# Second half's value products by query halves into two banks, and the first half's turn into the banks of the main products

## The chip, the cores and the metric

The kernel runs on one core of one Trainium2 chip. Its time is the device time in microseconds (us) of one execution; below it, all times are from one execution that the hardware profiler recorded, counted from its first instruction. TensorE (PE) multiplies and writes to PSUM, which has eight banks of 512 float32 values in each of 128 partitions; VectorE (DVE) and ScalarE (ACT) read PSUM and write SBUF; GpSimd (POOL) and SyncE (SP) mostly issue transfers.

## The reference

A trunk of two layers over 256 tokens of width 2048: a Mamba-2 layer, then a layer of sliding-window attention with a sink per head. Only the attention is touched by the change:

```python
WINDOW = 128; ATT_HEADS = 32; KV_HEADS = 4; ATT_HEAD_DIM = 64
qb = q.reshape(bsz, nb, WINDOW, hk, rq, hd)                      # nb = 2 blocks of 128 tokens
kk = concat([previous block's keys, own keys]); vv = likewise    # 256 keys a block
s = einsum("bcqhrd,bckhd->bchrqk", qb, kk) * hd ** -0.5
diff = (arange(128)[:, None] + 128) - arange(256)[None, :]
valid = (diff >= 0) & (diff < WINDOW) & (key exists)
s = where(valid, s, -inf)
m = maximum(max(s), sink); p = exp(s - m)
p = p / (sum(p) + exp(sink - m))
o = einsum("bchrqk,bckhd->bcqhrd", p, vv)
return (o * silu(gate)) @ w_out
```

A token sees itself and the 127 tokens before it. So a query of the second block (tokens 128 to 255) sees exactly 128 keys: query i of the block sees keys i+1 to 127 of the first block and keys 0 to i of its own. For the queries 0 to 63 of the block no key above 63 of the own block counts, and for the queries 64 to 127 no key below 64 (in truth 65) of the first.

## The kernel before

All large products keep float32 accuracy by splitting both operands into a high and a low float32r part and adding three products (`mac`, `out_unit`, `x_stat`; lines L248, L319 to L321, L972). Weights stream in by SyncE's queue as units of 128 x 2048 values; ScalarE makes the high part (`wh`, L160) and VectorE the low part (`wl`, L163). Main products write to PSUM tiles of the pool `mm`, which has four banks that rotate; everything else (turns, scores, value products) writes to the pool `ax`, with the other four. A new tile takes the bank of the tile four places earlier in its pool and so waits for that tile's readers.

The attention layer works by four head groups j (one key/value head, eight query heads) and two halves h of the tokens (`attend`). The order of large blocks is written out in `B_ORDER`: q product, gate product and output product of the groups, q and gate of group 1 ahead of the output of group 0 and so on. The attention steps are hung between the main products by `later(n, fn)`, which runs a step n units of main products later; on each engine the instructions then keep the order that a scheduler gives them. For one group and half the steps are:

- q is turned (`qtr`, L1050) into `qT`, with two heads above each other in the 128 partitions.
- Scores (L1087): the two heads of a partition pair are products with 64 rows, `par` 0 in rows 0 to 63 and `par` 1 in rows 64 to 127, into two ax tiles. The first half takes two ax tiles (four heads each, 128 keys). The second half takes four (two heads each, 256 keys).
- For the second half, ScalarE copies the own block's scores to `p` (L1101), and VectorE puts the first block's over them where the own key lies in the future (L1102). So `p` holds 128 keys a query, each at its place in one block or the other. Softmax follows on VectorE and ScalarE.
- `turn_p` turns `p` by 128 x 128 transposes (L1127), four to a PSUM tile. For the first half a tile is copied out, one by VectorE (L1138) and one by ScalarE (L1136). For the second half VectorE writes it twice, masked by `anti` (first block's keys) and by `tri` (own keys) (L1131).
- `pv` multiplies values and turned `p` (L1145), 64 output columns to a product, `par` 0 to partitions 0 to 63 and `par` 1 to partitions 64 to 127 of one ax tile, over 512 moving columns (four heads x 128 queries). The first half has two such products, the second half four, two by blocks of keys. VectorE multiplies with the gate (L1151), ScalarE and VectorE split the result (L1160, L1161) for the output product.

In groups 0 to 2 the second half's scores come directly behind the first half's turn on TensorE; in group 3 the first half's turn comes later, directly ahead of the second half's turn. The second half's value products stand ahead of the next group's `qtr` in groups 0 to 2, and directly behind the first half's in group 3.

The values `vt` and the turned `p` are plain float32, and such a product shows as two matmul records in the trace.

Of the kernel before, what the change touches and what calls it, by code (L numbers as in the profile page):

```python
# [8 lines left out]
F32 = mybir.dt.float32  # L9
# [5 lines left out]
ALU = mybir.AluOpType  # L15
AX = mybir.AxisListType

P = 128
# [63 lines left out]
def trunk(ctx: ExitStack, tc: tile.TileContext, A: dict, out: bass.AP, dbg=None):  # L82
    nc = tc.nc
    PSUM = bass.MemoryType.PSUM

    def pool(name, bufs=1, side=None, space=None, stack=ctx):
        kw = {"space": space} if space is not None else {}
        return stack.enter_context(
            tc.tile_pool(name=name, bufs=bufs, side=side, reuse_waits="tile", **kw)
        )  # L90
# [9 lines left out]
    def nm(s):  # L100
        uid[0] += 1
        return f"{s}_{uid[0]}"

    def mm_tile():
        return mm_ps.tile([P, 512], F32, tag="mm", name=nm("mm"), bufs=4)

    def ax_tile():
        return ax_ps.tile([P, 512], F32, tag="ax", name=nm("ax"), bufs=4)
# [145 lines left out]
    def later(n, fn):  # L254
        pending.append([n, fn])
# [547 lines left out]
    for g in range(NG):  # L803
        t = 10 * g
# [136 lines left out]
    bp = pool("bp")  # L941
# [38 lines left out]
    vt = bp.tile([P, 2, S], F32, tag="vt", name="vt")  # L980
# [49 lines left out]
    sg = {}  # L1030
# [44 lines left out]
    def attend(j, h):  # L1075


        nk = P * (h + 1)
        q2 = qT[j, h]
        p = bp.tile([P, 8, P], F32, tag=f"p{h}", name=nm("p"), bufs=1)  # L1080
        per = 512 // nk
        for b in range(0, 4, per):
            pss = [ax_tile(), ax_tile()]
            for i in range(per):
                for par in range(2):
                    rows = slice(64 * par, 64 * par + 64)
                    nc.tensor.matmul(  # L1087
                        pss[par][:, i * nk : (i + 1) * nk], q2[rows, b + i, :], kT[rows, j, :nk],
                        start=True, stop=True,
                    )  # L1090
            for par in range(2):
                v = p[:, par * 4 + b : par * 4 + b + per, :]
                if h == 0:
                    nc.vector.tensor_tensor(
                        v, pss[par][:].rearrange("p (a k) -> p a k", a=per),
                        mask_a0.unsqueeze(1).to_broadcast([P, per, P]), ALU.add,
                    )
                    continue
                two = pss[par][:].rearrange("p (a c k) -> p a c k", a=per, c=2)

                nc.scalar.copy(v, two[:, :, 1, :])  # L1101
                nc.vector.copy_predicated(  # L1102
                    v, mask_a0.bitcast(U32).unsqueeze(1).to_broadcast([P, per, P]), two[:, :, 0, :]
                )
        sk = snk[:, j * 8 : j * 8 + 8]
        sm = bp.tile([P, 8, 8], F32, tag="sm", name=nm("sm"), bufs=2)
        mx, ng, rs, es, ri = [sm[:, i, :] for i in range(5)]
        nc.vector.tensor_reduce(mx, p[:], AX.X, ALU.max)
        nc.vector.tensor_tensor(mx, mx, sk, ALU.max)
        nc.vector.tensor_scalar(ng, mx, -1.0, None, ALU.mult)  # L1110
        nc.vector.tensor_tensor(es, sk, ng, ALU.add)
        nc.scalar.activation(es, es, AF.Exp)
        for r in range(8):
            nc.scalar.activation(
                p[:, r, :], p[:, r, :], AF.Exp, bias=ng[:, r : r + 1], accum_out=rs[:, r : r + 1]
            )
        nc.vector.tensor_tensor(rs, rs, es, ALU.add)
        nc.vector.reciprocal(ri, rs)
        nc.vector.tensor_tensor(p[:], p[:], ri.unsqueeze(2).to_broadcast([P, 8, P]), ALU.mult)

        pts = {}

        def turn_p():
            for par in range(2):
                pt = ax_tile()
                for a in range(4):
                    nc.tensor.transpose(pt[:, a * P : (a + 1) * P], p[:, par * 4 + a, :], ident)  # L1127
                for kc in range(h + 1):
                    t = bp.tile([P, 512], F32, tag="pt", name=nm("pt"), bufs=NPT)
                    if h:  # L1130
                        nc.vector.tensor_tensor(  # L1131
                            t[:].rearrange("p (a q) -> p a q", a=4), pt[:].rearrange("p (a q) -> p a q", a=4),
                            (anti, tri)[kc].unsqueeze(1).to_broadcast([P, 4, P]), ALU.mult,
                        )
                    elif par:
                        nc.scalar.copy(t[:], pt[:])  # L1136
                    else:
                        nc.vector.tensor_copy(t[:], pt[:])  # L1138
                    pts[kc, par] = t

        def pv():
            ov = ax_tile()
            for kc in range(h + 1):
                for par in range(2):
                    nc.tensor.matmul(  # L1145
                        ov[64 * par : 64 * par + 64, :], vt[:, kc, j * 64 : j * 64 + 64], pts[kc, par][:],
                        start=kc == 0, stop=kc == h,
                    )
            o = bp.tile([P, 4, P], F32, tag="o", name=nm("o"), bufs=1)
            hs = slice(h * P, (h + 1) * P)  # L1150
            nc.vector.scalar_tensor_tensor(  # L1151
                o[:], ov[:].rearrange("p (a t) -> p a t", a=4), 0.5, sg[j][:, :, hs], ALU.mult, ALU.mult
            )
            if j not in os_:
                os_[j] = (
                    bp.tile([P, 4, S], F32R, tag="oH", name=nm("oH"), bufs=2),
                    bp.tile([P, 4, S], F32R, tag="oL", name=nm("oL"), bufs=2),
                )
            oH, oL = os_[j]
            nc.scalar.activation(oH[:, :, hs], o[:], AF.Copy)  # L1160
            nc.vector.tensor_tensor(oL[:, :, hs], o[:], oH[:, :, hs].bitcast(F32), ALU.subtract)  # L1161


        last = j == 3
        later(4 if last and h == 0 else 3, turn_p)
        later((5 if last else 6) if h == 0 else (8 if 0 < j < 3 else 4), pv)
        if h == 0:
            later(1 if last else 3, lambda: attend(j, 1))
# [193 lines left out]
```

## Time and profile before

| | us |
|---|---|
| median of 3 runs (lowest, highest) | 998.05 (997.94, 998.2) |
| span of the profiled execution | 996.5 |
| TensorE busy (its share of the span) | 990.9 (99%) |
| VectorE busy | 771.6 (77%) |
| ScalarE busy | 567.2 (57%) |
| GpSimd busy | 106.4 (11%) |
| score products L1087, 128 records | 14.7 |
| value products L1145, 48 records | 11.8 |
| transposes of p L1127, 64 records | 8.3 |

For the profiled execution the profile gives the span, from the first to the last instruction, and no other time of its own; the runs' times include what lies around the span, 1.55 us by the median. Busy times of TensorE count each record with its drain, and records overlap: a better measure of what a group costs is the time from its first start to the start of the next line's first record. In the timeline, consecutive records of one line are merged, with their count behind an x. "128*64 128x512" is a product with 128 rows and 64 columns of the array and 512 moving columns.

### The profile page before, as it was taken

The numbers are of one execution on the slowest core, as the hardware profiler recorded it, in microseconds if no ns is written. First come the engines' busy times: TensorE is split into PE (matmuls) and PEld (weight loads), VectorE is DVE, ScalarE is ACT, GpSimd is POOL, SyncE is SP. The second block draws the span as 40 slices with busy tenths as digits, with TensorE's granted clock in tenths as the row PEclk, the third lists the DMA queues.
The fourth block names the chain that finished last, engine by engine and source line by source line (L and its number), as shares of the span: only waits on it lengthen the run. The fifth ranks groups of instructions, "written<-read, shape, count | busy, mean of one in ns | idle before, by whom it ended". The sixth has DMA issues, their size and how long they took to land.

```text
span 996.5 us, 17887 instructions
## 1 busy us (share of the span) xinstructions
PE 990.9 (99%) x7036; PEld 899.3 (90%) x7036; DVE 771.6 (77%) x1186; ACT 567.2 (57%) x992; POOL 106.4 (11%) x130
## 2 busy tenths in 40 slices
PE   9999999999999999999999999999999999999998
PEld 8999989999999998999999999888988878978976
DVE  7888897867886886786786787898688776676686
ACT  7595856547646645664654764565545544544542
POOL 0001202004003003000300300403000000000003
PEclk9999999999999999999999999999999999999999
DMA  9787587565576666656656456457664546546432
GB/s 364 250 281 300 168 275 213 183 221 178 181 243 184 222 196 192 212 191 210 207 172 227 152 188 219 169 169 244 234 199 144 177 155 192 154 150 200 133 145 84
DMA packets 61555, 198.81 MB, mean 200 GB/s; under 512 B 6848, under 2 KB 11360, under 8 KB 61216
## 3 DMA queue, kind: packets, MB, share of 16 engines
q1 hardware_dynamic: 58528, 188.47, 57.6%
q0 software_dynamic: 2336, 8.69, 2.6%
q8 instruction: 55, 0.90, 0.4%
q10 hardware_dynamic: 608, 0.52, 0.2%
q14 instruction: 28, 0.23, 0.1%
HBM read 195.43 MB, written 2.23 MB: 198 GB/s over the span
## 4 chain that ended last, share of the span: by engine, by line
PE 98%; DVE 1%; issue 0%; ACT 0%; DVEq 0%
PE mm L248 53%; PE mm L972 10%; PE mm L319 9%; PE mm L320 9%; PE mm L321 9%; PE ax L627 2%; PE ax L1087 1%; PE ax L1145 1%; PE ax L603 1%; PE ax L1127 1%; PE ax L586 0%; PE mm L386 0%; PE ax L1050 0%; PE ax L903 0%; DVE wl L163 0%; PE ax L368 0%
## 5 line engine op out<-in xcount | busy, mean ns | idle before, releaser
L163 DVE TENSOR_TENSOR wl<-wr,wh 128x1024 fp32r<-128x1024 f32 (+2 forms) x338 | 392.9, 1182 | 108.7 <-ACT wh L160 106.6
L160 ACT ACTIVATE wh<-wr 128x1024 fp32r<-128x1024 f32 (+2 forms) x338 | 332.6, 1010 | 208.4 <-issue 84.9
L248 PE MATMUL mm<-xH,wh 128*128 128x256 f32 x1280 | 355.7, 278 | 0.0
L248 PE MATMUL mm<-xL,wh 128*128 128x256 f32 x1280 | 354.4, 277 | 0.0
L248 PE MATMUL mm<-xH,wl 128*128 128x256 f32 x1280 | 354.2, 277 | 0.0
L248 PEld LDWEIGHTS mm<-xH,wh 128*128 128x128 f32 x1280 | 241.0, 188 | 1.8 <-ACT wh L194 0.5
L248 PEld LDWEIGHTS mm<-xL,wh 128*128 128x128 f32 x1280 | 241.0, 188 | 1.0
L248 PEld LDWEIGHTS mm<-xH,wl 128*128 128x128 f32 x1280 | 240.8, 188 | 0.0
L319 PE MATMUL mm<-wh,yH 128*128 128x512 f32 x256 | 101.4, 396 | 0.0
L320 PE MATMUL mm<-wh,yL 128*128 128x512 f32 x256 | 99.8, 390 | 0.0
L321 PE MATMUL mm<-wl,yH 128*128 128x512 f32 x256 | 99.7, 389 | 0.0
L643 POOL TENSOR_TENSOR yz<-yz,z 128x256 f32<-128x256 f32 x32 | 32.8, 1033 | 470.4 <-DVE yz L638 470.4
L248 PE MATMUL mm<-x1H,wh 128*128 128x256 f32 x256 | 71.7, 280 | 0.0
L490 DVE SCALAR_TENSOR_TENSOR cv<-mm,pc,cv 128x255 f32<-128x255 f32 x144 | 68.6, 477 | 3.3 <-ACT cv L488 1.9
L248 PE MATMUL mm<-x1L,wh 128*128 128x256 f32 x256 | 70.8, 277 | 0.0
L248 PE MATMUL mm<-x1H,wl 128*128 128x256 f32 x256 | 70.8, 276 | 0.0
L972 PE MATMUL mm<-wh,x1H 128*128 128x512 f32 x160 | 62.9, 393 | 0.0
L972 PE MATMUL mm<-wl,x1H 128*128 128x512 f32 x160 | 61.8, 389 | 0.0
L972 PE MATMUL mm<-wh,x1L 128*128 128x512 f32 x160 | 60.9, 390 | 0.0
L319 PEld LDWEIGHTS mm<-wh,yH 128*128 128x128 f32 x256 | 48.1, 188 | 10.3 <-DVE z L579 1.0
L321 PEld LDWEIGHTS mm<-wl,yH 128*128 128x128 f32 x256 | 48.1, 188 | 10.2
L320 PEld LDWEIGHTS mm<-wh,yL 128*128 128x128 f32 x256 | 48.1, 188 | 9.0
(217 smaller groups left out, 1349.6 us busy)
## 6 DMA issues: line engine op xcount, KB each, us to landing
wr<-in_wa SPq DMA_DIRECT2D x154, 512.0 KB, 5.0
wr<-in_wo SPq DMA_DIRECT2D x64, 512.0 KB, 4.2
wr<-in_wq SPq DMA_DIRECT2D x32, 512.0 KB, 4.5
wr<-in_wg SPq DMA_DIRECT2D x31, 512.0 KB, 4.9
wr<-in_wb SPq DMA_DIRECT2D x16, 512.0 KB, 4.8
wr<-in_wb SPq DMA_DIRECT2D x32, 256.0 KB, 3.6
rb<-rscr SPq DMA_DIRECT2D x11, 512.0 KB, 4.6
wr<-in_wkv SPq DMA_DIRECT2D x8, 512.0 KB, 4.5
```

Source lines behind the costliest of these rows:

```text
L160: m = nc.scalar.activation(h[:, sl], v, AF.Copy)
L163: m = nc.vector.tensor_tensor(l[:, sl], v, h[:, sl].bitcast(F32), ALU.subtract)
L248: m = nc.tensor.matmul(ps, a, b, start=first and i == 0, stop=last and i == 2)
L319: pinned(nc.tensor.matmul(ps, aH[:, k, hs], u.h[:, ks], start=k == 0 and add is None, stop=False), pin)
L320: pinned(nc.tensor.matmul(ps, aL[:, k, hs], u.h[:, ks], start=False, stop=False), pin)
L321: pinned(nc.tensor.matmul(ps, aH[:, k, hs], u.l[:, ks], start=False, stop=k == 3), pin)
L490: nc.vector.scalar_tensor_tensor(a[:, sft:], ps[:, : S - sft], w(3 - sft), a[:, sft:], ALU.mult, ALU.add)
L603: nc.tensor.transpose(ps[:, o : o + P], st.xs[i][:, c * P : (c + 1) * P], ident)
L627: nc.tensor.matmul(ps[64 * r : 64 * r + 64, cols], xd[:, c, r, :], e[:, 256:] if c else e[:, :256], start=c == 0, stop=c == 1,)
L643: nc.gpsimd.tensor_tensor(v, v, st.z[i][:], ALU.mult)
L972: m = nc.tensor.matmul(ps[:], (x1H, x1L, x1H)[i][:, kk, hs], (u.h, u.h, u.l)[i][:, ks], start=(kk, i) == (0, 0), stop=ui == 3 and (k, i) = ...
L1087: nc.tensor.matmul(pss[par][:, i * nk : (i + 1) * nk], q2[rows, b + i, :], kT[rows, j, :nk], start=True, stop=True,)
```

## The change

For the second half, the four value products over 512 columns become eight over 256 columns (four heads x 64 queries). Each half of the queries has a PSUM tile of its own (`ovs[0]`, `ovs[1]`, 256 columns each, from the ax pool). First come the products that need all 128 keys: first block's keys for the queries 0 to 63, own keys for the queries 64 to 127. Then those that need 64 keys: own keys 0 to 63 for the queries 0 to 63, first block's keys 64 to 127 for the queries 64 to 127. The multiplication with the gate becomes two instructions, one for each tile. The first half's value products stay as they were. The other edit lets the first half's turn of `p` write to tiles of the mm pool instead of the ax pool.

```diff
         def turn_p():
             for par in range(2):
-                pt = ax_tile()
+                pt = ax_tile() if h else mm_tile()
                 for a in range(4):
                     nc.tensor.transpose(pt[:, a * P : (a + 1) * P], p[:, par * 4 + a, :], ident)
...
         def pv():
-            ov = ax_tile()
-            for kc in range(h + 1):
+            o = bp.tile([P, 4, P], F32, tag="o", name=nm("o"), bufs=1)
+            hs = slice(h * P, (h + 1) * P)
+            vs = slice(j * 64, j * 64 + 64)
+            if h == 0:
+                ov = ax_tile()
                 for par in range(2):
                     nc.tensor.matmul(
-                        ov[64 * par : 64 * par + 64, :], vt[:, kc, j * 64 : j * 64 + 64], pts[kc, par][:],
-                        start=kc == 0, stop=kc == h,
+                        ov[64 * par : 64 * par + 64, :], vt[:, 0, vs], pts[0, par][:], start=True, stop=True
                     )
-            o = bp.tile([P, 4, P], F32, tag="o", name=nm("o"), bufs=1)
-            hs = slice(h * P, (h + 1) * P)
-            nc.vector.scalar_tensor_tensor(
-                o[:], ov[:].rearrange("p (a t) -> p a t", a=4), 0.5, sg[j][:, :, hs], ALU.mult, ALU.mult
-            )
+                nc.vector.scalar_tensor_tensor(
+                    o[:], ov[:].rearrange("p (a t) -> p a t", a=4), 0.5, sg[j][:, :, hs], ALU.mult, ALU.mult
+                )
+            else:
+
+                ovs = [ax_tile()[:, :256].rearrange("p (a t) -> p a t", a=4) for _ in range(2)]
+
+                def pt_of(kc, par, rows, part):
+                    t = pts[kc, par][:].rearrange("p (a t) -> p a t", a=4)
+                    return t[rows, :, 64 * part : 64 * part + 64]
+
+                whole = slice(0, P)
+                for part in range(2):
+                    for par in range(2):
+                        nc.tensor.matmul(
+                            ovs[part][64 * par : 64 * par + 64], vt[:, part, vs], pt_of(part, par, whole, part),
+                            start=True, stop=False,
+                        )
+                for par in range(2):
+                    for part in range(2):
+                        rows = slice(64 * part, 64 * part + 64)
+                        nc.tensor.matmul(
+                            ovs[part][64 * par : 64 * par + 64], vt[rows, 1 - part, vs],
+                            pt_of(1 - part, par, rows, part), start=False, stop=True,
+                        )
+                for part in range(2):
+                    ts_ = slice(h * P + 64 * part, h * P + 64 * part + 64)
+                    nc.vector.scalar_tensor_tensor(
+                        o[:, :, 64 * part : 64 * part + 64], ovs[part], 0.5, sg[j][:, :, ts_], ALU.mult, ALU.mult
+                    )
```

## The prediction

> **What bounds the kernel now.** I read the page first, then the chain of waits, then the timeline of TensorE around the lines the change touches, then the waits of that line, and last the timelines of VectorE and ScalarE for the moments at which PSUM banks come free.
>
> ```profile
> span 996.5 us, 17887 instructions
> ...
> PE 990.9 (99%) x7036; PEld 899.3 (90%) x7036; DVE 771.6 (77%) x1186; ACT 567.2 (57%) x992; POOL 106.4 (11%) x130
> ...
> PEclk9999999999999999999999999999999999999999
> ...
> PE 98%; DVE 1%; issue 0%; ACT 0%; DVEq 0%
> ```
>
> TensorE is busy for 99% of the span at the full granted clock, and 98% of the chain is its own work. So the time is the sum of TensorE's own durations and its few stalls: what is taken from that row, and not given back in a stall, leaves the total. The profiled span of 996.5 us stands 1.55 us below the median of the runs, 998.05; I subtract the same gain from both.
>
> The second half's score products (L1087, 64-row stationary tiles in pairs, four banks) show the one place where TensorE stalls in the attention part. Timeline of TensorE: start, length with drain, line, output and inputs, count.
>
> ```profile
> 739.23 2.79 PE L1087 MATMUL ax<-kT,qT 64*128 64x256 f32 x16
> 741.95 0.50 PE L972 MATMUL mm<-wh,x1H 128*128 128x512 f32 x1
> ...
> 792.94 2.71 PE L1087 MATMUL ax<-kT,qT 64*128 64x256 f32 x16
> 795.58 0.50 PE L319 MATMUL mm<-wh,oH 128*128 128x512 f32 x1
> ...
> 868.35 2.71 PE L1087 MATMUL ax<-kT,qT 64*128 64x256 f32 x16
> 870.99 0.50 PE L319 MATMUL mm<-wh,oH 128*128 128x512 f32 x1
> ...
> 931.98 2.00 PE L1087 MATMUL ax<-kT,qT 64*128 64x256 f32 x16
> 933.90 0.39 PE L248 MATMUL mm<-x1H,wh 128*128 128x256 f32 x1
> ```
>
> From start to the next line's start the same 16 records take 741.95 - 739.23 = 2.72, 2.64 and 2.64 us in head groups 0, 1, 2, but 1.92 in group 3, where no turn of the first half stands just ahead. The waits, and the two readers of that turn, say why:
>
> ```profile
> PEld ax L1087 <- ACT pt L1136: 0.8, 2, 0.4
> PEld ax L1087 <- DVE pt L1138: 0.5, 1, 0.5
> ...
> 739.75 0.68 DVE L1138 COPY pt<-ax 128x512 f32<-128x512 f32 x1
> ...
> 740.28 0.56 ACT L1136 COPY pt<-ax 128x512 f32<-128x512 f32 x1
> ```
>
> The turn has filled two of the four ax banks; the third and fourth score tiles wait until L1138 and L1136 have copied them out.
>
> **Part 1: the first half's turn goes to mm banks.** Its eight transposes stay where they are, as long as they were; the compiled order of every engine is the same as before except for the instructions replaced. The scores then find four free ax banks (their holders four tiles earlier are the q transposes and the first half's scores, read long before). If groups 0 to 2 take what group 3 takes, the gain is (2.72 - 1.92) + 2 x (2.64 - 1.92) = 2.24 us. In group 3 the turn stands beside the second half's turn and nothing waits on it: gain 0.
>
> The cost could be a new wait on the mm banks, since four rotate for main products and every later tile now follows the one two places nearer. The tight places, by end of read against first write:
>
> ```profile
> 758.73 0.68 DVE L1044 TENSOR_TENSOR qt<-mm,bias 128x512 f32<-128x512 f32 x1
> ...
> 760.37 0.37 PE L248 MATMUL mm<-x1H,wh 128*128 128x256 f32 x1
> ...
> 864.74 0.41 DVE L1071 SCALAR_TENSOR_TENSOR sg<-sg,mm 128x256 f32<-128x256 f32 x1
> ...
> 867.39 1.03 PE L1127 MATMUL ax<-cc,p 128*128 128x128 f32 x8
> ...
> 949.88 0.68 DVE L330 TENSOR_TENSOR xr<-xr,mm 128x512 f32<-128x512 f32 x1
> ...
> 952.04 0.48 PE L319 MATMUL mm<-wh,oH 128*128 128x512 f32 x1
> ```
>
> - The first gate product of group 1 takes the bank of group 1's q product, read until 758.73 + 0.68 = 759.41. It starts at 760.37 now and at 759.57 once 0.80 is gained: 0.16 us to spare, if VectorE's row doesn't move. Cost 0; if VectorE slips, what it slips beyond 0.16, once.
> - The second turn tile of group 2 (about 867.8, the fifth of eight transposes) takes a gate's bank, read until 865.15. By then some 2.7 us are gained; the gate's readers follow TensorE's own product and move with it. Cost 0, bound 0.1.
> - In group 3 an output product at 952.04 takes a bank read until 950.56. Cost 0: both move together.
>
> **Part 2: the second half's value products.** Before, four products of 128 keys x 64 columns over 512 moving columns; each is two records (two passes of an f32 product), and the two column halves of the array run at once.
>
> ```profile
> 59.73 0.59 PE L586 MATMUL ax<-ct,bt 128*128 128x256 f32 x2
> 60.16 0.38 PE L587 MATMUL ax<-ct,bt 128*128 128x128 f32 x2
> ...
> 766.02 1.94 PE L1145 MATMUL ax<-pt,vt 128*64 128x512 f32 x8
> 767.88 1.09 PE L1050 MATMUL ax<-cc,qt 128*128 128x128 f32 x8
> ...
> 957.67 2.80 PE L1145 MATMUL ax<-pt,vt 128*64 128x512 f32 x12
> 960.39 0.50 PE L319 MATMUL mm<-wh,oH 128*128 128x512 f32 x1
> ```
>
> Twelve records take 960.39 - 957.67 = 2.72 us, eight 1.86: four records are 0.86, so a pass over 512 columns is 0.43 and always carries two records; 4 x 0.43 leaves 0.14 of the 1.86 for entering and leaving this tile shape. A full-array product of 256 columns (L586) is two passes in 0.43, 0.215 each: a pass costs by its moving columns, not by rows or columns of the array used. The scores agree: sixteen records of 64-row tiles, two at a time, are 8 x 0.215 = 1.72, and 0.20 for entering and leaving.
>
> After, there are eight products of 256 columns. The first four (128 keys, L1165 of the changed file) are 4 passes of two records: 0.86, with 0.14 for the shape. The other four (L1172) have 64 keys and 64 output columns each: four different quarters of the array, into two banks.
>
> - If all four run at once: 2 passes, 0.43, and 0.20 for the second shape (price of the scores' rows). Sum 0.86 + 0.14 + 0.43 + 0.20 = 1.63 us against 1.86: gain 0.23.
> - If only two run at once: 4 passes, 0.86; sum 2.06, loss 0.20.
> - If none overlaps: 8 passes, 1.72; sum 2.92, loss 1.06.
>
> The trace shows pairs side by side along rows (L1087) and along columns (L1145), never four quarters. I take four: both splits work alone, and two windows inside group 0's scores, where the second tile's bank was late, show one record running in 740.60 to 740.75 and three by 740.92:
>
> ```profile
> 740.49 0.48 PE L1087 MATMUL ax<-kT,qT 64*128 64x256 f32 x1
> ...
> 740.49 0.89 PE L1087 MATMUL ax<-kT,qT 64*128 64x256 f32 x3
> ```
>
> One tile went on while its neighbour was held, and the two then ran out of step, so the tiles look independent of each other. The change of shape lies between 0 (free: 1.43, gain 0.43) and twice 0.20 (1.83, gain 0.03). Four head groups: 4 x 0.23 = 0.92 us, from 0.1 to 1.7.
>
> A page of the Trainium skill weighs against this part: "TensorE: Matmul & The Clock Gate", in its closing table, says that a product with a small contraction takes the same time as a full one and gains only by tiles that run together. The rows of L586 and L1087 agree (0.215 either way); by that rule alone, with no four-tile overlap, the sum is one of the two losses above. The same page's Part 3 gives about 4 ns per extra tile in a pack; as an estimate from that figure four quarters would cost some 0.01 us more a pass, 0.1 us in all.
>
> Four more VectorE instructions come with it (the gate's multiplication in halves):
>
> ```profile
> L1071 DVE SCALAR_TENSOR_TENSOR sg<-sg,mm 128x256 f32<-128x256 f32 x16 | 6.4, 401 | 1.4 <-ACT sg L1070 1.4
> ...
> L1151 DVE SCALAR_TENSOR_TENSOR o<-ax,sg 128x512 f32<-128x512 f32 x8 | 5.5, 684 | 0.1
> ...
> 761.32 0.68 DVE L1151 SCALAR_TENSOR_TENSOR o<-ax,sg 128x512 f32<-128x512 f32 x1
> ...
> 964.07 0.68 DVE L1161 TENSOR_TENSOR oL<-o,oH 128x512 fp32r<-128x512 f32 x1
> ...
> 966.21 0.39 PE L320 MATMUL mm<-wh,oL 128*128 128x512 f32 x1
> ```
>
> Two of 0.40 for one of 0.68 is 0.12 us each, cost 0 in the total: the earliest user is the last output block, which reads at 966.21 what is done at 964.75; 1.46 us less 0.12 and less the 0.23 by which TensorE comes earlier leaves 1.1. The eight more weight loads per head group run under the passes, as now. The second tile's bank last held the first half's value tile, which L1151 reads from 761.32 to 762.00 against a start at 766.02 in group 0; groups 1 and 2 have longer between them, and in group 3 the bank was the turn's, whose readers make the operands: cost 0.
>
> **Sum.** 2.24 + 0.92 = 3.16 us: span 996.5 to 993.3, median 998.05 to 994.9.
>
> **The rivals.** A, four quarters run at once: 994.9, between 994.1 (free change of shape) and 995.7 (double). B, only two at once: -2.24 + 4 x 0.20 = -1.44, so 996.6; for it, that no row shows four; against it, the independent tiles. C, the other side: the quarters don't overlap at all, 4 x 1.06 - 2.24 = +2.0, so 1000.1. It turns slower than before from a second half of 1.86 + 2.24 / 4 = 2.42 us on, six passes where I count two; against it both kinds of pairs. D, the turn's gain doesn't come, because the scores still wait (for a bank, or for the mm tiles behind the gate's readers): only 0.92 is left, 997.1; for it the 0.16 us of spare time in group 1, against it that such a slip is paid once and not three times.
>
> **Chances.** A 0.71, B 0.13, C 0.06, D 0.10. About 0.2%, 2.0 us, can be told from no change, so A is faster (below 996.05), B and D are the same, C stands at the edge: I give it to slower. Faster 0.72, same 0.20, slower 0.08. The range of A alone is 994.1 to 995.7; with B it is 993.9 to 996.8, which takes in the free change of shape and B's own uncertainty.
>
> **What would show it.** The score groups of L1087 at 1.92 us in all four head groups, and no wait of L1087 for L1138 or L1136 (part 1). The eight first-phase records in 0.86 to 1.0 us and the eight of L1172 starting four together, 0.215 apart, with the whole second half at 1.63 (part 2, A); pairs 0.215 apart in four steps would be B, single records C. The first gate product of group 1 with idle time behind L1044 would be D's beginning. The prediction is wrong if TensorE shows a new stall at an mm tile, or if the change of shape costs several times 0.2.

## The result and the profile after

The changed kernel takes 994.73 us (median of 7 runs, 994.1 to 995.64) against 997.94 for the kernel before, run beside it: 3.2 us less, a ratio of 0.9964 (95% interval 0.9954 to 0.9973). The runs of the two kernels don't overlap (the kernel before took 997.38 to 999.32). The forecast was 994.9 us, 3.16 us less. A second comparison on another occasion gave 994.99 against 997.94, 0.9970 (0.9959 to 0.9981).

The page of the profile after, the lines that answer to those of before:

```profile
span 992.6 us, 17959 instructions
...
PE 987.1 (99%) x7068; PEld 898.7 (91%) x7068; DVE 772.1 (78%) x1190; ACT 566.6 (57%) x992; POOL 105.9 (11%) x130
...
PE 99%; DVE 0%; DVEq 0%; issue 0%
```

TensorE still bounds everything; it is busy 3.8 us less. Of the 3.9 us between the two spans, 0.7 lies ahead of the first instruction that differs (the q transposes of head group 0 start at 714.23 before and 713.54 after): that is chance of one execution. The rest, 3.2 us, agrees with the runs.

The second half's scores in the four head groups, in the timeline of TensorE after:

```profile
738.53 2.00 PE L1087 MATMUL ax<-kT,qT 64*128 64x256 f32 x16
740.46 0.50 PE L972 MATMUL mm<-wh,x1H 128*128 128x512 f32 x1
...
791.25 2.00 PE L1087 MATMUL ax<-kT,qT 64*128 64x256 f32 x16
793.18 0.50 PE L319 MATMUL mm<-wh,oH 128*128 128x512 f32 x1
...
865.69 2.00 PE L1087 MATMUL ax<-kT,qT 64*128 64x256 f32 x16
867.62 0.50 PE L319 MATMUL mm<-wh,oH 128*128 128x512 f32 x1
...
928.33 2.00 PE L1087 MATMUL ax<-kT,qT 64*128 64x256 f32 x16
930.26 0.39 PE L248 MATMUL mm<-x1H,wh 128*128 128x256 f32 x1
```

All take 1.93 us from start to the next line's start, as group 3 did before. The waits of L1087 for the turn's readers are gone; what is left of it in the list of waits is below 0.3 us in a row and names neither L1136 nor L1138.

The value products, group 0 and group 3 (L1148 is the first half, L1165 the products with 128 keys, L1172 those with 64):

```profile
764.53 1.08 PE L1165 MATMUL ax<-pt,vt 128*64 128x256 f32 x8
765.54 0.66 PE L1172 MATMUL ax<-pt,vt 64*64 64x256 f32 x8
766.14 1.17 PE L1050 MATMUL ax<-cc,qt 128*128 128x128 f32 x8
...
954.02 1.08 PE L1148 MATMUL ax<-pt,vt 128*64 128x512 f32 x4
954.93 1.03 PE L1165 MATMUL ax<-pt,vt 128*64 128x256 f32 x8
955.89 0.66 PE L1172 MATMUL ax<-pt,vt 64*64 64x256 f32 x8
956.49 0.50 PE L319 MATMUL mm<-wh,oH 128*128 128x512 f32 x1
```

The second half's value group takes 766.14 - 764.53 = 1.61 us instead of 1.86, and both halves together in group 3 take 2.47 instead of 2.72. The eight L1172 records, two passes of four quarters, fit in 766.14 - 765.54 = 0.60 us, the change of shape behind them included; in the trace the four records of a pass start 0.007 us apart.

One new wait appeared. The q transposes (L1050) of group 0 are eight of 0.11 us; the row after has 1.17 us where before had 1.09. The second four need VectorE's second q half:

```profile
766.18 0.21 DVE L961 TENSOR_TENSOR qt<-rt 128x64 f32<-128x64 f32 x1
766.32 0.21 DVE L962 TENSOR_TENSOR qt<-rt 128x64 f32<-128x64 f32 x1
```

L962 ends at 766.53. The fifth transpose would be due at 766.14 + 0.16 + 3 x 0.11 = 766.63 and starts at 766.68, 0.15 us behind that end; the group is 0.08 us longer. TensorE had come forward by 1.74 us here (767.88 to 766.14), 0.69 of it the chance seen above. VectorE, busy without a break from the end of the softmax on, had come forward by 0.15 only. Before, the same instruction ended 1.2 us ahead of the first transpose:

```profile
766.46 0.22 DVE L962 TENSOR_TENSOR qt<-rt 128x64 f32<-128x64 f32 x1
```

What holds VectorE back is a transfer. L1021, a step of the residual that stands between the copies of the second half's scores on VectorE, reads a parameter row (`gb`) that GpSimd fetches (L1019). Before, then after:

```profile
739.20 0.54 POOL L1019 DMA_DIRECT2D gb<-in_lng  x1 [27.07 <-DVE xr L1021]
744.41 0.69 DVE L1021 TENSOR_TENSOR xr<-xr,gb 128x512 f32<-128x512 f32 x1 [1.15 <-DMA gb<-in_lng]
...
738.50 0.54 POOL L1019 DMA_DIRECT2D gb<-in_lng  x1 [26.86 <-DVE xr L1021]
744.28 0.69 DVE L1021 TENSOR_TENSOR xr<-xr,gb 128x512 f32<-128x512 f32 x1 [1.72 <-DMA gb<-in_lng]
```

From the start of its issue to L1021 it took 5.21 us before and 5.78 after, and in both executions L962 ends 22.26 to 22.27 us after L1021 starts. So VectorE's place here is set by the moment at which this transfer lands.

### The profile page after: what moved, and what is told of

The parts are those of the page before. It is cut to its first block, busy times and chain, and to the rows that moved or that the text cites. A ratio compares the mean times of both kernels' runs of the same rounds, so it can differ in the third digit from the quotient of the medians.

```text
span 992.6 us, 17959 instructions
## 1 busy us (share of the span) xinstructions
PE 987.1 (99%) x7068; PEld 898.7 (91%) x7068; DVE 772.1 (78%) x1190; ACT 566.6 (57%) x992; POOL 105.9 (11%) x130
## 4 chain that ended last, share of the span: by engine, by line
PE 99%; DVE 0%; DVEq 0%; issue 0%
PE mm L248 53%; PE mm L972 11%; PE mm L319 9%; PE mm L320 9%; PE mm L321 9%; PE ax L627 2%; PE ax L1087 1%; PE ax L603 1%; PE ax L586 0%; PE mm L386 0%; PE ax L1148 0%; PE ax L1050 0%; PE ax L1127 0%; PE ax L1165 0%; PE mm L1127 0%; PE ax L903 0%
## 5 line engine op out<-in xcount | busy, mean ns | idle before, releaser
L248 PE MATMUL mm<-xH,wh 128*128 128x256 f32 x1280 | 355.4, 278 | 0.0
L248 PE MATMUL mm<-xL,wh 128*128 128x256 f32 x1280 | 354.1, 277 | 0.0
L248 PE MATMUL mm<-xH,wl 128*128 128x256 f32 x1280 | 353.9, 276 | 0.0
L248 PEld LDWEIGHTS mm<-xH,wh 128*128 128x128 f32 x1280 | 240.7, 188 | 1.8 <-ACT wh L194 0.5
L248 PEld LDWEIGHTS mm<-xL,wh 128*128 128x128 f32 x1280 | 240.8, 188 | 1.0
L248 PEld LDWEIGHTS mm<-xH,wl 128*128 128x128 f32 x1280 | 240.7, 188 | 0.0
L248 PE MATMUL mm<-x1H,wh 128*128 128x256 f32 x256 | 71.7, 280 | 0.0
L248 PE MATMUL mm<-x1L,wh 128*128 128x256 f32 x256 | 70.8, 277 | 0.0
L248 PE MATMUL mm<-x1H,wl 128*128 128x256 f32 x256 | 70.8, 276 | 0.0
```

Of the source, the lines that this page charges most:

```text
L248: m = nc.tensor.matmul(ps, a, b, start=first and i == 0, stop=last and i == 2)
```

## The experiments

The theory on trial is that two separate gains add: 2.2 us from the turn's banks (no stall of the scores) and 1.05 us from the value products (four quarters of the array at once), less a small wait. Where a kernel is said to be beside the kernel before, both ran on the same chip in one comparison.

**The turn alone.**

```diff
-                pt = ax_tile()
+                pt = ax_tile() if h else mm_tile()
```

> Only the first half's turn goes to the mm banks; the second half's value products stay as before. Theory (the two edits are separate and add): the second half's scores L1087 take 1.93 us in all four head groups, with no wait for the readers of the turn, and the value products stay at 1.87; the time is 2.2 us below the kernel before, about 995.7 beside 997.9. Rival (most of the 3.2 us comes from the value products and their banks, the turn's move only shifts the wait to an mm tile): within 1 us of the kernel before, with idle time of TensorE at a main product behind a turn.

Measured: 996.1 us against 997.88, ratio 0.9981 (0.9972 to 0.9989), so 1.8 us less by the medians, 0.9 to 2.8 by the interval. Its scores and values in group 0:

```profile
738.85 2.00 PE L1087 MATMUL ax<-kT,qT 64*128 64x256 f32 x16
740.77 0.50 PE L972 MATMUL mm<-wh,x1H 128*128 128x512 f32 x1
...
764.84 1.94 PE L1145 MATMUL ax<-pt,vt 128*64 128x512 f32 x8
766.71 0.55 PE L1050 MATMUL ax<-cc,qt 128*128 128x128 f32 x3
```

The scores take 1.92 us, and the values 1.87 as before. Groups 1 and 2 repeat it, and no main product behind a turn has idle time ahead of it. Counted from the q transposes of group 0 to the end of the profile, which leaves out the chance ahead of them, this kernel takes 280.15 us (994.0 - 713.85) against 282.27 (996.5 - 714.23): 2.1 us less. The theory holds, the rival falls.

**The value products alone.** The turn goes back to the ax banks.

```diff
-                pt = ax_tile() if h else mm_tile()
+                pt = ax_tile()
```

> Only the second half's value products are changed; the first half's turn stays in the ax banks. Theory: the value groups take 1.61 us instead of 1.87 (2.46 instead of 2.73 in head group 3), the scores still wait for L1138 and L1136 and take 2.72, 2.64 and 2.64 us; the time is 4 x 0.26 = 1.05 us below before, about 996.9. Rival (the two new tiles in the ax pool crowd it, and the gain of the values shows only because the turn left the pool): a new wait at a q transpose or a score tile and a time within 0.5 us of before.

Measured: 996.78 against 997.88, ratio 0.9987 (0.9978 to 0.9996), 1.1 us less by the medians. Timeline, then its list of waits:

```profile
738.62 2.79 PE L1087 MATMUL ax<-kT,qT 64*128 64x256 f32 x16
741.34 0.50 PE L972 MATMUL mm<-wh,x1H 128*128 128x512 f32 x1
...
765.38 1.08 PE L1165 MATMUL ax<-pt,vt 128*64 128x256 f32 x8
766.39 0.66 PE L1172 MATMUL ax<-pt,vt 64*64 64x256 f32 x8
766.98 0.44 PE L1050 MATMUL ax<-cc,qt 128*128 128x128 f32 x2
```

```profile
PEld ax L1087 <- ACT pt L1136: 0.8, 2, 0.4
...
PEld ax L1087 <- DVE pt L1138: 0.5, 1, 0.5
```

The stall of the scores is back at 2.72 us with the same two names, and the values take 1.60 us. The gains are separate: 1.8 and 1.1 us by medians against 3.2 and 3.0 for both, and by the profiles from the q transposes of group 0 on 2.1 and 1.1 (994.8 - 713.62 = 281.18) against 3.2 (992.6 - 713.54 = 279.06).

**All keys in the second phase.** This keeps the two banks, the halves of the queries and the short passes, and takes only the quarters away.

```diff
-                        rows = slice(64 * part, 64 * part + 64)
+                        rows = whole
```

> As the changed kernel, but the four products of the second phase use all 128 keys instead of 64 (the rows added are zeros of the mask), so two array halves side by side instead of four quarters. Theory (the value products gain only because four quarters run at once): 8 passes of 0.215 and 0.14 for one shape, 1.86 us a group, so 1.05 us above the changed kernel, about 995.8. Rival (the gain comes from the two banks, the shorter passes or the split of the reading, and not from the quarters): 1.61 us a group and the time of the changed kernel, about 994.7.

Measured: 995.81 against 997.88, ratio 0.9981 (0.9972 to 0.9990), the same ratio as the turn alone.

```profile
764.15 1.08 PE L1165 MATMUL ax<-pt,vt 128*64 128x256 f32 x8
765.06 1.08 PE L1172 MATMUL ax<-pt,vt 128*64 128x256 f32 x8
766.07 0.44 PE L1050 MATMUL ax<-cc,qt 128*128 128x128 f32 x2
```

The value group takes 1.92 us, 0.06 more than the 1.86 expected, so the whole gain of the value products is gone: it comes from the quarters alone. The 0.06 appears together with the order of the products: in the second phase the two that follow one another use the same half of the array, and their passes start 0.05 us out of step where those of the first phase start 0.007 apart.

**The quarters between the two 128-key pairs.** Same products and tiles, one more change of the tile shape.

```diff
-                for part in range(2):
-                    for par in range(2):
-                        nc.tensor.matmul(... whole ..., start=True, stop=False)
+                full(0)
                 for par in range(2):
                     for part in range(2):
...
+                            pt_of(1 - part, par, rows, part), start=part == 1, stop=part == 0,
...
+                full(1)
```

> As the changed kernel, same products and tiles, but the four quarter products stand between the two pairs of 128-key products, so TensorE changes its tile shape once more in each value group. Theory (a change of shape costs about 0.15 us: 0.10 at the last pass before it and 0.05 at the first behind it): 1.76 us a value group and 0.6 us above the changed kernel, about 995.3. Rival 1 (the price is the 0.20 of the scores' rows): 1.81 a group, 0.8 us more. Rival 2 (the drain is only paid towards full-array work): 1.61 a group and no difference.

Measured: 995.78 against 997.88, ratio 0.9978 (0.9969 to 0.9987); the changed kernel's interval, 0.9954 to 0.9973, overlaps it slightly. The value group in the trace:

```profile
764.71 0.65 PE L1166 MATMUL ax<-pt,vt 128*64 128x256 f32 x4
765.29 0.66 PE L1175 MATMUL ax<-pt,vt 64*64 64x256 f32 x8
765.88 0.65 PE L1166 MATMUL ax<-pt,vt 128*64 128x256 f32 x4
766.47 0.33 PE L1050 MATMUL ax<-cc,qt 128*128 128x128 f32 x1
```

1.76 us a group where the changed kernel has 1.61: one more change of shape costs 0.15 us, the theory's number. In the group itself rivals 1 (0.20) and 2 (free) fall.

The time as a whole is a miss. It is 2.1 us below the kernel before, where the changed kernel is 3.2 below: 1.1 us lost where the theory had 0.6. The other half lies behind the q transposes, in the first gate products of groups 0 to 2. Here are 16 of the 48 records of L248 in group 0 (shortest, median and longest in ns), in the changed kernel and in this one:

```profile
L248 PE MATMUL mm<-x1L,wh x16: 276/276/281, 767.3 to 772.4; 128*128 128x256 f32 x16
...
L248 PE MATMUL mm<-x1L,wh x16: 281/282/282, 767.5 to 772.8; 128*128 128x256 f32 x16
```

The 48 records follow one another 0.118 us apart instead of 0.113 and take 5.83 us instead of 5.63, in all three groups: 3 x 0.20 us on top of 4 x 0.15. The granted clock is 1.00 in both, and the profile shows no idle time of TensorE there. Why they are slower is not shown.

**The changed kernel again,** beside the two that follow.

> The changed kernel once more, beside the next two. Every theory: 3.2 us below the kernel before. The q transposes of head group 0 (L1050) took 0.93 us in its profile instead of 0.85; if that is a wait for VectorE's second q half (L962), it returns here, and if it was chance of one execution, it doesn't.

Measured: 994.99 against 997.94.

```profile
764.77 1.17 PE L1165 MATMUL ax<-pt,vt 128*64 128x256 f32 x8
765.87 0.66 PE L1172 MATMUL ax<-pt,vt 64*64 64x256 f32 x8
766.46 1.23 PE L1050 MATMUL ax<-cc,qt 128*128 128x128 f32 x8
```

The wait returned, 0.14 us at the q transposes, and 0.09 at the value products (765.87 - 764.77 = 1.10 where the first profile has 1.01), whose fourth product needs the last of VectorE's masked copies, here ready at 763.96 + 1.28 = 765.24:

```profile
763.96 1.28 DVE L1131 TENSOR_TENSOR pt<-ax,cc 128x512 f32<-128x512 f32 x2
```

So the wait is no chance of one execution, but its size hangs on when the transfer for L1021 lands, and that differs by up to 0.9 us between profiles. In all seven profiles whose VectorE waits for it, L962 ends 22.26 to 22.27 us after L1021 starts. VectorE's lead is the time from the end of L962 to the moment at which the fifth transpose is due; below 0.15 us of it there is a wait.

| kernel | issue of the transfer to L1021, us | VectorE's lead, us | wait of the q transposes, us |
|---|---|---|---|
| before | 5.21 | 1.70 | 0 |
| turn alone | 5.53 | 0.58 | 0 |
| values alone | 6.06 | 0.55 | 0 |
| all keys | 5.31 | 0.86 | 0 |
| quarters between | 5.18 | 0.83 | 0 |
| changed, first profile | 5.78 | 0.10 | 0.08 |
| changed, again | 5.91 | 0.04 | 0.14 |

Both gains together bring TensorE 1.05 us forward in group 0. As an estimate from these rows, with a landing as early as before (5.21) the changed kernel would have had a lead of some 0.67 us and no wait, and the turn alone with the latest landing (6.06) some 0.05 us and a wait. That it takes both gains to make TensorE wait is therefore not shown.

**The scores cut the same way.** If four quarters run at once for the value products, they should for the scores: a query half needs 192 of the 256 keys.

```diff
+                    if h:
+                        for part in range(2):
+                            qs = slice(64 * part, 64 * part + 64)
+                            nc.tensor.matmul(
+                                pss[par][qs, i * nk + 64 * part : i * nk + 64 * part + 192],
+                                q2[rows, b + i, qs], kT[rows, j, 64 * part : 64 * part + 192],
+                                start=True, stop=True,
+                            )
+                        continue
...
-                nc.scalar.copy(v, two[:, :, 1, :])
-                nc.vector.copy_predicated(v, mask_a0 ..., two[:, :, 0, :])
+                up, dn, k0, k1 = slice(0, 64), slice(64, P), slice(0, 64), slice(64, P)
+                nc.scalar.copy(v[:, :, k0], two[:, :, 1, k0])
+                nc.scalar.copy(v[dn, :, k1], two[dn, :, 1, k1])
+                nc.scalar.copy(v[up, :, k1], two[up, :, 0, k1])
+                for r, k in ((up, k0), (dn, k1)):
+                    m = mask_a0[r, k].bitcast(U32).unsqueeze(1).to_broadcast([64, per, 64])
+                    nc.vector.copy_predicated(v[r, :, k], m, two[r, :, 0, k])
```

> As the changed kernel, and the second half's scores are cut the same way: queries 0 to 63 against keys 0 to 191, queries 64 to 127 against keys 64 to 255, four quarters of the array at once over 192 moving columns instead of two halves over 256. The copies behind them are split, ScalarE gets one more piece and VectorE two half-size ones for each it had. Theory (a pass costs by its moving columns as long as the tiles differ, with four as with two): 8 x 0.16 + 0.20 = 1.49 us a score group instead of 1.93, 4 x 0.44 = 1.8 us below the changed kernel, about 993.0. Rival 1 (twice the weight loads bound the passes): 1.93 or more a group, no gain. Rival 2 (the split copies make softmax late in head group 0, and TensorE waits there): 1.49 a group, but a wait of over 0.5 us at the turn or the q transposes of group 0.

Measured: 993.18 us (992.62 to 993.32) against 997.94, ratio 0.9952 (0.9939 to 0.9964), and 1.8 us below the changed kernel of the same comparison.

```profile
739.11 1.53 PE L1090 MATMUL ax<-kT,qT 64*64 64x192 f32 x32
740.57 0.50 PE L972 MATMUL mm<-wh,x1H 128*128 128x512 f32 x1
...
766.25 1.09 PE L1050 MATMUL ax<-cc,qt 128*128 128x128 f32 x8
```

1.46 us a score group, in all four. Thirty-two records with their weight loads run in eight passes of 0.16 us, so rival 1 falls. The q transposes of group 0 don't wait at all, so rival 2 does not show in this form. The copies now stand ahead of L1021 on VectorE, and L1021 starts at 744.89, 0.35 us after its transfer landed at 744.54, so VectorE no longer idles for it. This is the fastest version of the study.

**The same with the extra copy on VectorE.**

```diff
-                nc.scalar.copy(v[up, :, k1], two[up, :, 0, k1])
+                nc.vector.tensor_copy(v[up, :, k1], two[up, :, 0, k1])
```

> As the run before it, but the extra copy is VectorE's: some 4 x 0.25 = 1 us more VectorE work in each head group. Theory (in head group 0 VectorE is busy without a break from softmax to the q transposes, and these already wait for it): score groups 1.49 as above, and the q transposes of group 0 wait up to 1 us more, so 0 to 1 us above the run before it. Rival (VectorE has room everywhere, since TensorE bounds): the same time as the run before it and no longer wait.

Measured: 993.54 against 997.94, ratio 0.9956 (0.9943 to 0.9968), 0.4 us above the run before it by the medians, with intervals that overlap. The trace is clear:

```profile
765.86 0.66 PE L1050 MATMUL ax<-cc,qt 128*128 128x128 f32 x4
766.96 0.63 PE L1050 MATMUL ax<-cc,qt 128*128 128x128 f32 x4 [0.44 <-DVE qt L962]
```

The second four transposes start 1.10 us after the first four, where 0.16 + 3 x 0.11 = 0.49 is their own time: a wait of 0.6 us for L962. Neither this run nor the one before it has VectorE waiting for the transfer of L1021; counted from the q transposes of head group 0, L962 ends 0.91 us later here, and the four extra copies are 0.28 us each. So the wait is the extra copies' doing, at the one place where VectorE is the late one. The rival, room everywhere, falls.

## Why the prediction was right, and where its working was not

- **The bound.** TensorE's own work set the time before and after, and what left it left the total. The sum of the parts by the trace is 0.79 + 0.71 + 0.71 = 2.21 us for the scores (forecast 2.24), 4 x 0.26 = 1.05 for the values (forecast 0.92), less 0.08 for the new wait (forecast 0): 3.18 us against 3.2 measured. That the forecast of 3.16 came so close is in part luck, because the three differences, -0.03, +0.13 and -0.08, nearly cancel.
- **Part 1** was right in place, mechanism and size: the turn alone gives it, and the two named waits are gone with it and return without it.
- **Part 2, four quarters at once.** Right, and shown by taking the quarters alone away: the value group goes from 1.61 to 1.92 us. The step that no row of before had shown, rival A against B and C, is settled for A.
- **Part 2, the change of shape.** Taken at 0.20 from the scores' rows; it measures 0.15. With that the group is 0.86 + 0.14 + 0.43 + 0.15 = 1.58 by the prediction's own sum, against 1.61 measured, where 1.63 stood.
- **The tight place in group 1 was wrong.** The prediction gave the first gate product the bank of the q product, with 0.16 us to spare, and the account of the kernel says that a new tile takes the bank of the tile four places earlier. It doesn't always. After the change, VectorE still reads the q product while the gate product writes:

```profile
758.59 0.68 DVE L1044 TENSOR_TENSOR qt<-mm,bias 128x512 f32<-128x512 f32 x1
...
758.88 0.37 PE L248 MATMUL mm<-x1H,wh 128*128 128x256 f32 x1
```

  The q product holds two of the four banks, the one being read here and one that is read only from 760.25 on. So the gate's tile lies in one of the two that the turn had used, whose readers L1138 and L1136 were done by 740.15, 18.7 us earlier. That fits a pool that hands out the bank which came free first; by what rule it does so, no run shows. So the moved turn made no main product wait, and the rival D had no ground there; the cost of 0 was right for another reason.
- **The step that did cost something** was one the prediction left at nothing: TensorE coming earlier in group 0, where VectorE's work hangs on the transfer for L1021 and doesn't move with TensorE. It looked for such a place among the banks and not among the operands. The q transposes' second operand had 1.7 us of lead (its L962 ended at 766.68 before, and the fifth transpose started 0.49 behind 767.88, at 768.37). The gain in this group, 0.79 + 0.26 = 1.05 us, used most of it, and in the profile after the transfer, which landed 0.57 us later behind its issue than before, used up nearly all the rest.
- No cost of VectorE's four more instructions or of the second tile's bank shows in the trace, as the prediction said; which bank that tile had, no run shows.
- **The Trainium skill's** rule of "TensorE: Matmul & The Clock Gate", closing table, that a product with a small contraction gains only by tiles that run together, agrees with the trace: the group with 64 keys and four quarters at once takes 1.61 us, and with 128 keys and two halves at once 1.92. The prediction let this rule weigh against part 2, since no row of before showed four tiles at once; with four at once it is the reason for the gain.

## What to carry to other kernels

When one engine bounds the whole time, look in the timeline for groups of equal work with unequal length. Here the difference was a stall with a name, and it came back in full when the turn got its banks elsewhere. Masked blocks are worth cutting to tiles only if the tiles then run side by side; a product with half the rows saved nothing alone here, and two along rows and two along columns ran together. One more change of tile shape cost 0.15 us in the group, and the gate products behind it ran slower as well, so products of one shape belong together. After such a gain check the operands of the next instructions as well as their buffers: another engine's lead is what the gain spends, and a single profile does not tell how long that lead is, since a transfer's landing moved it by up to 0.9 us here.

## What the runs showed of the hardware

Four quarters of the array take a pass of 256 moving columns in 0.22 us ((0.60 - 0.15) / 2), as two halves or the whole array do, and one of 192 columns in 0.16 with the four weight loads of a pass hidden. With two products in a row on the same half of the array the two halves fell 0.05 us out of step, 0.06 us a group, where alternating halves start 0.007 us apart. Whether that is the order alone wasn't tried separately. The transfer for L1021 took 5.2 to 6.1 us from its issue to its reader's start in the seven profiles in which the reader waited for it.
